# Delta net's inverse: 32x32 block products over all 128 rows, with zeros in the other rows

## The chip, the cores and the metric

The kernel runs on one core of a Trainium2 chip. The metric is the time of one execution on the device in microseconds (us). A core has five engines, each with its own instruction stream: TensorE (PE in the profile; PEld is its loading of the stationary operand), VectorE (DVE), ScalarE (ACT), GpSimd (POOL) and SyncE (SP). TensorE multiplies with a contraction over the partitions of its two operands: `pm(out, lhsT, rhs)` sums over the rows (partitions) that the slices of `lhsT` and `rhs` name, the columns of `lhsT` become the rows of `out`, and the columns of `rhs` its columns. A product "32x32 over 32 rows" therefore has 32 rows of contraction, 32 output rows and 32 output columns.

## The reference

The program is a trunk of two blocks on a sequence of 1024 rows and 1024 columns: a gated delta net and a convolutional feed-forward net, then retention and a second feed-forward net. The change lies in the delta net, which has 8 heads of 128 columns and works on chunks of 64 rows. For each head and chunk it solves a lower triangular system with a unit diagonal:

```
kk  = jnp.where(strict, jnp.einsum('bhncd,bhnmd->bhncm', kb, k) * decay, 0.0)
rhs = jnp.concatenate([v * beta[..., None], kb * jnp.exp(gc)[..., None]], axis=-1)
sol = lax.linalg.triangular_solve(kk + eye, rhs, left_side=True, lower=True, unit_diagonal=True)
u, w = sol[..., :dv], sol[..., dv:]
```

Then a scan over the 16 chunks carries a 128x128 state from chunk to chunk.

## The kernel before, in words

Two chunks of 64 rows are held as one tile of 128 rows, so a head has 8 chunk pairs, n = 0..7 (`NCH`). Heads are worked in quads (g = 0, 1, four heads) and pairs (p = 0..3, two heads). The inverse of the 64x64 triangles is built from the inside out.

`t_path(g)` makes, for the four heads of a quad, the inverses of all 32x32 diagonal blocks by 31 steps of forward substitution on DVE. They lie in two "lane" tiles, RX and TX (one the transpose of the other, block by block; L900, L904).

`t_chain(p)` (L915) then joins 32x32 blocks to 64x64 and 64x64 to 128x128 for the two heads of a pair. Its stages, which the prediction goes through:

- R, the result, is zeroed by POOL (L922), and its four diagonal blocks are copied from RX (`block`, L930 on DVE for odd p, L932 on ACT for even p; POOL L952 for the lower two).
- T0, a lane tile of 128 rows x (2 heads, 8 chunk pairs, 64 columns), gets three diagonal blocks from TX: blocks 0 and 2 into columns 0:32 and block 1 into columns 32:64 (L930 or L932). POOL zeroes the corner in rows 0:32, columns 32:64 (L937).
- First products (L960 to L965): 32 per pair, U^T times T0, 32x32 over 32 rows, into the PSUM tile `pa`. Each is fp32 and appears as two instructions in the profile, `mm<-T,U 32*32`.
- ACT copies `pa` to `xa` (L967), rows 32:64 and 96:128.
- Second products (L970 to L977): 48 per pair, `xa` with R and R with `xa`, 32x32 over 32 rows, into `pb`; for o = 0 two alternate that write different column groups of the array. In the profile they are `mm<-R,xa 32*32` and `mm<-xa,R 32*32`.
- DVE writes them, negated, into T0 (L980) and R (L984).
- Then the same with blocks of 64: products `mm<-T,U 64*64` over 64 rows, ACT's copy `xb` (L994), products `mm<-R,xb 64*64`, and R is written.

What the delta net needs around it runs between these stages: `prep(p)` (transposes of V by products with the identity, `acc<-cst,qkv` L719 on PE, L1017 on DVE), `dt_half` (`acc<-qkv` products, DVE L1046), `conv_half` (the causal convolution of a projection: ACT L485 and L488 read the PSUM accumulator, DVE L490 three taps, ACT L491 silu), the projections themselves (gemm "triples" of three 128x512 products, `acc<-hT,wl` and twice `acc<-hT,wh`), and `scan` (its steps over the chunks).

The order of the work on PE is set by a list scheduler in the program. `run(todo)` (L727) keeps a list of generators by priority. `pm` (L715) and `ptr` (L718) pin each product behind the one before it and advance a modelled clock; `yield LAT[..]` parks a generator for a modelled latency, `emit` and `after_ev` tie generators to each other, and `take` and `give` count free buffers ("lane": 4, "t2": 3, and others). Where no stage is ready, a filler (gemm triples) is issued. The order on the other engines follows from the program's dependencies by the tile scheduler, in about the order in which the operations are written.

Of the kernel before, what the change touches and what calls it, by code (L numbers as in the profile page):

```python
# [33 lines left out]
def trunk_kernel(ctx: ExitStack, tc, A):  # L34
    nc = tc.nc
    pe, act, dve, pool, sp = nc.tensor, nc.scalar, nc.vector, nc.gpsimd, nc.sync
# [9 lines left out]
    def tl(tag, shape, dt=F32, name=None):  # L46
        return sb.tile(shape, dt, tag=tag, name=name or tag, bufs=BUFS[tag])

    def two(tag, dt=F32, name=None):
        if tag in ("qkv", "auh"):  # L50
            return tl(tag, [P, HALF], dt, name), tl(tag, [P, HALF], dt, name)
        t = tl(tag, [P, 2, HALF], dt, name)
        return t[:, 0], t[:, 1]
# [7 lines left out]
    def mm_tile():  # L61
        return ps.tile([P, HALF], F32, tag="mm", name="mm", bufs=2)
# [13 lines left out]
    def v4(ap):  # L76
        return ap.rearrange("p (c f) -> p c f", f=P)
# [620 lines left out]
    U, DT, R, St = {}, {}, {}, {}  # L698
# [4 lines left out]
    events = {}  # L703

    def pq(inst, cost):
        if pin[0] is not None:
            tc.add_manual_dep(inst.ins, pin[0].name,
                              mybir.DependencyInfo(mybir.DependencyClass.NoSync, mybir.DependencyReason.DATA),
                              reason="issue order")
        pin[0] = inst.ins  # L710
        clk[0] += cost
# [3 lines left out]
    def pm(out, lhsT, rhs, start=True, stop=True, cost=None):  # L715
        pq(pe.matmul(out, lhsT, rhs, start=start, stop=stop), cost or COST[out.shape[-1]])  # L716
# [4 lines left out]
    def after_ev(*names):  # L721
        return ("ev", names)

    def emit(name, lat=0.0):
        events[name] = clk[0] + lat
# [40 lines left out]
    def q4s(q4):  # L766
        return slice(q4 * 4, (q4 + 1) * 4)
# [3 lines left out]
    def take(tag, n):  # L771
        while free[tag] < n:
            yield lambda: free[tag] >= n
        free[tag] -= n

    def give(tag, n):
        free[tag] += n
# [131 lines left out]
    def rx(h, n):  # L909
        return R[h][n // 4][:, n % 4 * P:n % 4 * P + P]  # L910
# [4 lines left out]
    def t_chain(p):  # L915
        heads = pairs[p]
        yield after_ev(("X", p // 2))
        yield from take("auh", 4)
        for h in heads:
            R[h] = two("auh", F32, "R")  # L920
            for q4 in range(2):
                pool.memset(R[h][q4], 0.0)  # L922
        yield after_ev(("T", p // 2))
        RX, TX = RTX[p // 2]
        cx = p % 2 * 16
        yield from take("lane", 1)

        def block(out, src):
            if p % 2:
                dve.tensor_copy(out, src)  # L930
            else:
                act.activation(out, src, AF.Copy)  # L932
        T0 = tl("lane", [P, 2, NCH, 64], name="T0")
        lo, hi = slice(0, 64), slice(64, 128)
        for hh, h in enumerate(heads):
            ch = slice(cx + hh * 8, cx + hh * 8 + 8)
            pool.memset(T0[0:32, hh, :, 32:64], 0.0)  # L937
            for b in range(3):
                bs = slice(32 * b, 32 * b + 32)
                cs = slice(32, 64) if b == 1 else slice(0, 32)  # L940
                block(T0[bs, hh, :, cs], TX[bs, :, ch].rearrange("p i c -> p c i"))
        for hh, h in enumerate(heads):
            for q4 in range(2):
                Rv = v4(R[h][q4])
                ch = slice(cx + hh * 8 + q4 * 4, cx + hh * 8 + q4 * 4 + 4)
                for b in range(4):
                    bs = slice(32 * b, 32 * b + 32)
                    src = RX[bs, :, ch].rearrange("p i c -> p c i")
                    if b < 2:
                        block(Rv[bs, :, bs], src)  # L950
                    else:
                        pool.tensor_copy(Rv[bs, :, bs], src)  # L952
        if ("T0", p ^ 1) in events:
            give("lane", 2)
        emit(("T0", p))
        yield LAT["T0"]
        yield from take("t2", 1)
        pa = mm_tile()
        xa = tl("t2", [P, HALF], name="xa")
        for o in (0, 64):  # L960
            l3, h3 = slice(o, o + 32), slice(o + 32, o + 64)
            for hh, h in enumerate(heads):
                for n in range(NCH):
                    c0 = hh * 256 + 32 * n
                    pm(pa[h3, c0:c0 + 32], U[h][l3, n, h3], T0[l3, hh, n, 0:32])  # L965
        for o in (0, 64):
            act.activation(xa[o + 32:o + 64], pa[o + 32:o + 64], AF.Copy)  # L967
        yield LAT["t1"]
        pb = mm_tile()
        for o in (0, 64):  # L970
            l3, h3 = slice(o, o + 32), slice(o + 32, o + 64)
            for hh, h in enumerate(heads):
                for n in range(NCH):
                    c0 = hh * 256 + 32 * n
                    pm(pb[l3, c0:c0 + 32], xa[h3, c0:c0 + 32], rx(h, n)[h3, h3])
                    if o == 0:
                        pm(pb[h3, c0:c0 + 32], rx(h, n)[h3, h3], xa[h3, c0:c0 + 32])  # L977
        for hh, h in enumerate(heads):
            pv = pb[:, hh * 256:hh * 256 + 256].rearrange("p (c f) -> p c f", f=32)
            dve.tensor_scalar(T0[32:64, hh, :, 0:32], pv[32:64], -1.0, None, ALU.mult)  # L980
            for o in (64, 0):
                l3, h3 = slice(o, o + 32), slice(o + 32, o + 64)
                for q4 in range(2):
                    dve.tensor_scalar(v4(R[h][q4])[l3, :, h3], pv[l3, q4s(q4)], -1.0, None, ALU.mult)  # L984
        give("t2", 1)
        yield LAT["t2"]
        yield from take("t2", 2)
        xb = {}
        for hh, h in enumerate(heads):
            pa = mm_tile()  # L990
            xb[h] = tl("t2", [P, HALF], name="xb")
            for n in range(NCH):
                pm(pa[hi, 64 * n:64 * n + 64], U[h][lo, n, hi], T0[lo, hh, n])
            act.activation(xb[h][hi], pa[hi], AF.Copy)  # L994
        emit(("Ufree", p))
        give("lane", 1)
        yield LAT["t3"]
        for h in heads:
            pb = mm_tile()
            for n in range(NCH):  # L1000
                pm(pb[lo, 64 * n:64 * n + 64], xb[h][hi, 64 * n:64 * n + 64], rx(h, n)[hi, hi])
            pv = pb.rearrange("p (c f) -> p c f", f=64)
            for q4 in range(2):
                dve.tensor_scalar(v4(R[h][q4])[lo, :, hi], pv[lo, q4s(q4)], -1.0, None, ALU.mult)
        give("t2", 2)
        emit(("R", p), LAT["mm"])
# [222 lines left out]
    c, z = "c", "z"  # L1229
# [5 lines left out]
    for p in range(4):  # L1235
        q = p & 2
        todo += [(q + 0.28, t_decay(p)), (q + 0.2, t_chain(p)), (q + 0.25, prep(p)), (q + 0.22, dt_half(p, 0)), (q + 0.24, dt_half(p, 1)),
                 (q + 0.0 + p % 2 * 0.1, scan(p, pairs[p][0])), (q + 0.05 + p % 2 * 0.1, scan(p, pairs[p][1]))]
# [577 lines left out]
    cs = {}  # L1816
# [358 lines left out]
```

## Time and profile before

| what | us |
|---|---|
| median of 3 runs | 2892.94 (2889.35 to 2898.21) |
| the profiled execution | 2895.01 |
| its span in the profile | 2893.2 |
| first 32x32 products, quad 0 / quad 1 | from 261.10 / from 507.09 |

The whole delta net inverse is two short stretches, one for each quad, in a span of 2893.2 us; the mean granted clock of TensorE over the span is 0.988. The views used are the page (busy shares, and the span in 40 slices, one slice being 72.3 us), the table by stretches, which gives for each stretch its length, the busy time of each engine with the number of instructions, the granted TensorE clock (PEclk, 1.00 is full speed), the DMA share and GB/s, and the waits, groups and timeline. In the table by stretches a row such as "257.64:261.05 3.41, 3.41 (x13) ..." reads: from 257.64 to 261.05, 3.41 us long, PE busy 3.41 us in 13 instructions. In groups and in the timeline, `L716` and `L719` are the two lines that issue every product here (`pm` and `ptr`), so products are told apart by the names of their tiles and their sizes. In the timeline a row has its start, its length and, in brackets, the idle time ahead of it with what ended it.

### The profile page before, as it was taken

To read this page: it belongs to the slowest core of one execution; us is meant where nothing else is said; L and a number is where in the kernel's file an instruction comes from. 1 tells how busy PE (TensorE), PEld (TensorE's weight loads), DVE (VectorE), ACT (ScalarE), POOL (GpSimd) and SP (SyncE) were. 2 spreads that over 40 slices of the span, in tenths; PEclk is the share of its full clock that TensorE was granted. 3 is DMA by queue.
4 is the path that set the end of the run, shared out by engine and by line. 5 is a ranking of instruction groups with operands and counts; after the bars stand their busy time and mean duration, and the time that the engine had idled before them with its cause. 6 is when DMAs were issued, how large, how long until landed. Compare 5 with 4: busy or idle time off the path is not lost.

```text
span 2893.2 us, 38921 instructions
## 1 busy us (share of the span) xinstructions
PE 2796.5 (97%) x13594; PEld 2289.9 (79%) x13594; DVE 2181.8 (75%) x3874; ACT 1296.7 (45%) x2387; POOL 484.6 (17%) x509
## 2 busy tenths in 40 slices
PE   7999999999999999999999999999999999999997
PEld 6788887887787777887788887777777788888886
DVE  5787688576788888858687666666789887777779
ACT  4664375344544444545443333222344644444543
POOL 0311231010022333000000001333301023332001
PEclk9998999899999999999999999999999999999999
DMA  7233233174254655845443354665764253434853
GB/s 277 84 99 117 89 129 112 44 241 153 83 179 169 204 181 176 294 150 175 150 142 113 131 197 143 203 188 177 233 221 150 73 197 138 142 132 161 289 182 116
DMA packets 252884, 465.30 MB, mean 161 GB/s; under 512 B 24144, under 2 KB 77776, under 8 KB 252688
## 3 DMA queue, kind: packets, MB, share of 16 engines
q1 hardware_dynamic: 218560, 408.02, 42.8%
q10 hardware_dynamic: 31488, 46.15, 4.3%
q0 software_dynamic: 2640, 8.65, 0.8%
q8 instruction: 107, 1.75, 0.2%
q14 instruction: 89, 0.73, 0.1%
HBM read 346.86 MB, written 115.87 MB: 160 GB/s over the span
## 4 chain that ended last, share of the span: by engine, by line
PE 60%; DVE 21%; DMA 8%; issue 5%; ACT 4%; POOL 1%; SPq 0%; ACTq 0%; DVEq 0%; POOLq 0%
PE acc L716 11%; PE acc L1292 5%; PE acc L1592 4%; PE sc L716 4%; PE acc L110 4%; PE acc L111 4%; PE acc L112 4%; PE mm L716 3%; PE sc L1292 3%; DVE o L1738 2%; DVE wb L90 2%; DMA wr<-in_ffn_up 2%; DMA mvw<-in_ada_w 2%; DVE mm L1346 2%; DVE ada L239 1%
## 5 line engine op out<-in xcount | busy, mean ns | idle before, releaser
L716 PE MATMUL acc<-hT,wh 128*128 128x512 f32 x960 | 301.1, 395 | 0.0
L1592 PE MATMUL acc<-bb,ab 128*128 128x512 f32 x984 | 231.0, 394 | 8.2 <-DVE ab L90 4.4
L89 ACT ACTIVATE ab<-ar 128x512 fp32r<-128x512 f32 x210 | 131.4, 630 | 222.9 <-PE mm L303 49.8
L1592 PEld LDWEIGHTS acc<-bb,ab 128*128 128x128 f32 x984 | 184.2, 189 | 50.0 <-DVE bb L90 4.7
L716 PEld LDWEIGHTS acc<-hT,wh 128*128 128x128 f32 x960 | 183.2, 191 | 36.1
L90 DVE TENSOR_TENSOR ab<-ar,ab 128x512 fp32r<-128x512 f32 x210 | 146.1, 701 | 80.3 <-ACT ab L89 80.1
L1292 PE MATMUL acc<-T,wb 128*128 128x512 f32 x840 | 202.0, 389 | 0.4 <-DVE wb L90 0.4
L716 PE MATMUL acc<-hT,wl 128*128 128x512 f32 x480 | 197.4, 411 | 3.3 <-ACT sq L509 2.1
L89 ACT ACTIVATE wb<-mm 128x512 fp32r<-128x512 f32 x216 | 124.3, 597 | 167.8 <-DVE mm L1346 154.1
L1292 PEld LDWEIGHTS acc<-T,wb 128*128 128x128 f32 x840 | 157.5, 188 | 33.8 <-ACT o L1739 1.2
L90 DVE TENSOR_TENSOR wl<-wr,wh 128x1024 fp32r<-128x1024 f32 x98 | 122.8, 1253 | 76.3 <-ACT wh L89 76.0
L90 DVE TENSOR_TENSOR wb<-wr,wb 128x512 fp32r<-128x512 f32 x162 | 116.3, 719 | 66.1 <-ACT wb L89 66.1
L89 ACT ACTIVATE wh<-wr 128x1024 fp32r<-128x1024 f32 x98 | 103.8, 1060 | 137.4 <-PE acc L716 54.1
L1769 POOL TENSOR_TENSOR o<-o 128x512 f32<-128x512 f32 x80 | 113.0, 1422 | 265.2 <-ACT pc L1362 173.1
L1738 DVE SCALAR_TENSOR_TENSOR o<-g,vc,o 128x512 f32<-128x512 f32 (+2 forms) x176 | 148.3, 852 | 8.2 <-ACT o L1733 7.0
L90 DVE TENSOR_TENSOR wb<-mm,wb 128x512 fp32r<-128x512 f32 x216 | 144.4, 681 | 7.6 <-ACT wb L89 7.6
L89 ACT ACTIVATE wb<-wr 128x512 fp32r<-128x512 f32 x162 | 101.2, 626 | 94.8 <-PE acc L1292 28.5
L1346 DVE TENSOR_TENSOR mm<-wr 128x512 f32<-128x512 f32 x108 | 85.9, 796 | 75.5 <-DMA wr<-in_ffn_up 60.9
L716 PE MATMUL acc<-wh,hT 128*128 128x512 f32 x384 | 134.3, 412 | 1.8 <-DVE vv L90 1.8
L1362 ACT ACTIVATE pc<-acc 128x512 f32<-128x512 f32 x143 | 84.3, 590 | 109.9 <-PE acc L1292 63.4
L239 DVE SCALAR_TENSOR_TENSOR ada<-mvw,e,ada 128x512 f32<-128x512 f32 x140 | 105.3, 752 | 23.4 <-DMA mvw<-in_ada_w 23.0
L110 PE MATMUL acc<-T,wb 128*128 128x512 f32 x292 | 114.4, 392 | 6.1 <-DVE wb L90 6.1
(674 smaller groups left out, 7371.9 us busy)
## 6 DMA issues: line engine op xcount, KB each, us to landing
wr<-in_ffn_up SPq DMA_DIRECT2D x92, 512.0 KB, 3.9
mvw<-in_ada_w SPq DMA_DIRECT2D x80, 512.0 KB, 4.3
ad<-o SPq DMA_DIRECT2D x154, 256.0 KB, 2.3
ar<-ad SPq DMA_DIRECT2D x154, 256.0 KB, 3.9
Br<-in_ffn_down SPq DMA_DIRECT2D x88, 256.0 KB, 3.6
wr<-in_ret_wv SPq DMA_DIRECT2D x32, 512.0 KB, 3.7
ar<-od SPq DMA_DIRECT2D x56, 256.0 KB, 5.2
wr<-in_gdn_wqkv SPq DMA_DIRECT2D x24, 512.0 KB, 3.6
```

What stands on the lines that cost most here:

```text
L89: anchor["sp"] = act.activation(dst_h, src, AF.Copy)
L90: eng.tensor_tensor(dst_l, src, dst_h, ALU.subtract)
L110: mm(acc, wl[:, k], hl[0], start=first, stop=False)
L111: mm(acc, wh[:, k], hl[1], start=False, stop=False)
L112: mm(acc, wh[:, k], hl[0], start=False, stop=last)
L239: dve.scalar_tensor_tensor(a, wr[:, kk], e[:, k:k + 1], a, ALU.mult, ALU.add)
L716: pq(pe.matmul(out, lhsT, rhs, start=start, stop=stop), cost or COST[out.shape[-1]])
L1292: return pe.matmul(*a, skip_group_check=True, **kw)
L1346: dve.tensor_tensor(t, x, y, op)
L1592: return pe.matmul(*args, skip_group_check=True, **kw)
L1738: dve.scalar_tensor_tensor(tv, gv[:, c0 - j:c1 - j], w[:, 2 - j:3 - j], tv, ALU.mult, ALU.add)
L1769: (dve if fp == 0 else pool).tensor_tensor(o[d], o[x], o[y], op)
```

## The change

T0 is zeroed whole, 128 rows, by POOL. Before the first products only blocks 0 and 2 are copied into it, block 0 into columns 0:32 and block 2 into columns 32:64. With that, the first products run over all 128 rows of U and T0: the rows of T0 that a product is not to see hold zeros in the columns that it uses. `xa` is zeroed whole by POOL (a new instruction for each pair), and ACT then fills the rows that it filled before. The second products run over all 128 rows of `xa` and R, with the zeros in `xa`. Block 1 of T0 (rows 32:64, columns 32:64) is copied behind the first products and ACT's copies, and the event "T1", with the return of two lane buffers, comes after it.

```diff
         for hh, h in enumerate(heads):
             ch = slice(cx + hh * 8, cx + hh * 8 + 8)
-            pool.memset(T0[0:32, hh, :, 32:64], 0.0)
-            for b in range(3):
+            pool.memset(T0[:, hh], 0.0)
+            for b in (0, 2):
                 bs = slice(32 * b, 32 * b + 32)
-                cs = slice(32, 64) if b == 1 else slice(0, 32)
-                block(T0[bs, hh, :, cs], TX[bs, :, ch].rearrange("p i c -> p c i"))
+                block(T0[bs, hh, :, 16 * b:16 * b + 32], TX[bs, :, ch].rearrange("p i c -> p c i"))
...
-        if ("T0", p ^ 1) in events:
-            give("lane", 2)
         emit(("T0", p))
...
         xa = tl("t2", [P, HALF], name="xa")
+        pool.memset(xa, 0.0)
         for o in (0, 64):
-            l3, h3 = slice(o, o + 32), slice(o + 32, o + 64)
+            h3 = slice(o + 32, o + 64)
...
-                    pm(pa[h3, c0:c0 + 32], U[h][l3, n, h3], T0[l3, hh, n, 0:32])
+                    pm(pa[h3, c0:c0 + 32], U[h][:, n, h3], T0[:, hh, n, o // 2:o // 2 + 32])
         for o in (0, 64):
             act.activation(xa[o + 32:o + 64], pa[o + 32:o + 64], AF.Copy)
+        for hh in range(2):
+            ch = slice(cx + hh * 8, cx + hh * 8 + 8)
+            block(T0[32:64, hh, :, 32:64], TX[32:64, :, ch].rearrange("p i c -> p c i"))
+        if ("T1", p ^ 1) in events:
+            give("lane", 2)
+        emit(("T1", p))
...
-                    pm(pb[l3, c0:c0 + 32], xa[h3, c0:c0 + 32], rx(h, n)[h3, h3])
+                    pm(pb[l3, c0:c0 + 32], xa[:, c0:c0 + 32], rx(h, n)[:, h3])
                     if o == 0:
-                        pm(pb[h3, c0:c0 + 32], rx(h, n)[h3, h3], xa[h3, c0:c0 + 32])
+                        pm(pb[h3, c0:c0 + 32], rx(h, n)[:, h3], xa[:, c0:c0 + 32])
```

The change also moves instructions, since the modelled clock and the buffer counts see it. On PE, in quad 0, the rows just ahead of the first products change as follows; `T_2178` is T0 of pair 0, `T_2203` (before) and `T_2201` (now) is T0 of pair 1, `acc<-qkv` are the products of `dt_half`, and `acc<-cst,qkv` the transposes of V.

```order
 L716 MATMUL acc<-hT,wh 128x512 x2
-L716 MATMUL acc<-qkv 128x128 x4
+L716 MATMUL acc<-hT,wl 128x512
+L716 MATMUL acc<-hT,wh 128x512 x2
+L719 MATMUL acc<-cst,qkv 128x128 x8
+L716 MATMUL acc<-hT,wl 128x512
+L716 MATMUL acc<-hT,wh 128x512 x2
 L716 MATMUL mm<-T_2178,U 32x32 x32
-L716 MATMUL mm<-T_2203,U 32x32 x32
+L716 MATMUL mm<-T_2201,U 32x32 x32
```

Four `dt_half` products leave this place, and two gemm triples and eight transposes come to it; the `dt_half` products stand further down, between the second products and the 64x64 products.

On ACT, at the same place in the program (quad 0, pair 0), the copies of T0's blocks and the convolution's steps stand as follows; `oq` is the convolution's output.

```order
 L488 ACTIVATE oq<-acc,vc 128x512
-L932 ACTIVATE T_2178<-TX 32x8x32 x6
 L491 ACTIVATE oq<-oq 128x512
-L1212 DMA qd<-oq 128x512
+L932 ACTIVATE T_2178<-TX 32x8x32 x2
+L1216 DMA qd<-oq 128x512
+L932 ACTIVATE T_2178<-TX 32x8x32 x2
+L491 ACTIVATE oq<-oq 128x512
 L485 ACTIVATE raw<-acc 128x512
 L488 ACTIVATE oq<-acc,vc 128x512
```

Where six copies stood ahead of the convolution's steps there are four, with a silu and the issue of a store among them; the two others come later, one ahead of each pair's copies of `xa`.

On ACT in quad 1, pair 2 (`T_4595` before and `T_4597` now are its T0), the same copies stand ahead of L251, which makes the shift and scale `ada` and frees its accumulator. Before, the rows there are these.

```order
L932 ACTIVATE T_4595<-TX 32x8x32 x5
L485 ACTIVATE raw<-acc 128x512
L488 ACTIVATE qkv<-acc,vc 128x512
L932 ACTIVATE T_4595<-TX 32x8x32
L491 ACTIVATE qkv<-qkv 128x512
L485 ACTIVATE raw<-acc 128x512
L488 ACTIVATE qkv<-acc,vc 128x512
L89 ACTIVATE wh<-wr 128x1024
L251 ACTIVATE ada,cs<-acc 128x128 x4
```

With the change they are these.

```order
L485 ACTIVATE raw<-acc 128x512
L488 ACTIVATE qkv<-acc,vc 128x512
L491 ACTIVATE qkv<-qkv 128x512
L932 ACTIVATE T_4597<-TX 32x8x32 x4
L485 ACTIVATE raw<-acc 128x512
L488 ACTIVATE qkv<-acc,vc 128x512
L89 ACTIVATE wh<-wr 128x1024
L251 ACTIVATE ada,cs<-acc 128x128 x4
```

The first L485, L488 and L491 come ahead of the copies, and four copies instead of six stand ahead of L251.

## The prediction

> **What bounds the kernel now.** I read the page first, for the engine that sets the span and for the clock of TensorE.
>
> ```profile
> span 2893.2 us, 38921 instructions
> PE 2796.5 (97%) x13594; PEld 2289.9 (79%) x13594; DVE 2181.8 (75%) x3874; ACT 1296.7 (45%) x2387; POOL 484.6 (17%) x509
> PEclk9998999899999999999999999999999999999999
> ```
>
> PE is busy for 97% of the span, so a microsecond taken out of PE's row, busy or idle, mostly leaves the span too; what becomes late on another engine counts only where it leaves PE idle. The second thing to see is the digit 8 in two of the 40 slices, the 4th and the 8th (216.9 to 289.3 and 506.3 to 578.6 us): there TensorE was granted less than its full clock for a while, and there the two quads do the products that the change rewrites. So I cut these places into stretches at the points where the clock changes, which turn out to lie 3.41 us apart.
>
> ```profile
> core 0: us, PE busy (x) PEld busy (x) DVE busy (x) ACT busy (x) POOL busy (x), PEclk, DMA share, GB/s
> 254.23:257.64 3.41, 0.99 (x7) 0.91 (x8) 2.28 (x4) 2.85 (x5) 0.00 (x0) 1.00 0.73 207
> 257.64:261.05 3.41, 3.41 (x13) 2.85 (x11) 3.18 (x5) 0.42 (x1) 0.00 (x0) 0.50 0.70 260
> 261.05:264.45 3.40, 3.40 (x116) 3.35 (x116) 1.76 (x3) 1.18 (x2) 0.00 (x0) 1.00 0.60 189
> 264.45:267.87 3.42, 3.42 (x29) 3.21 (x26) 1.26 (x2) 1.81 (x3) 0.00 (x0) 0.50 0.52 200
> 267.87:271.28 3.41, 3.41 (x171) 3.06 (x170) 1.02 (x4) 0.00 (x0) 0.00 (x0) 1.00 0.43 145
> 271.28:281.52 10.24, 9.56 (x76) 8.57 (x74) 6.63 (x21) 1.18 (x2) 0.00 (x0) 0.50 0.17 57
> 284.93:288.35 3.42, 3.42 (x49) 3.25 (x48) 1.05 (x3) 1.18 (x2) 0.00 (x0) 1.00 0.07 28
> 506.79:510.20 3.41, 3.41 (x111) 3.24 (x110) 1.09 (x3) 2.61 (x11) 0.00 (x0) 1.00 0.02 5
> 510.20:530.68 20.48, 19.80 (x282) 18.13 (x279) 8.91 (x25) 2.58 (x5) 0.00 (x0) 0.50 0.09 28
> ```
>
> Each row's clock answers to the row above it. After the nearly idle 254.23 to 257.64 (PE busy 0.99 of 3.41) comes a window at 0.50. But after 261.05 to 264.45, in which PE was busy all the time, comes a window at 0.50 as well, and so again after 267.87 to 271.28 and after 506.79 to 510.20. What those three share is over 100 small instructions: the 32x32 products. They keep PE busy and are followed by half a clock, as if PE had idled. Wider work does not do this: 284.93 to 288.35, most of it 64x64 products, stays at 1.00. So the clock seems to follow how much of the array works, and a 32x32 product over 32 rows counts as next to nothing. In 271.28 to 281.52 and 510.20 to 530.68 the same half clock lasts for three and for six windows.
>
> Last, the waits of PE, first around quad 0 (250 to 300), then around quad 1 (484 to 600).
>
> ```profile
> PE acc L719 <- ACT oq L488: 4.2, 1, 4.2
> ...
> PE acc L716 <- ACT ada L251: 1.1, 1, 1.1
> ...
> PE sc L716 <- ACT qkv L1079: 0.6, 1, 0.6
> ...
> PE sc L716 <- DVE qkv L1097: 0.3, 1, 0.3
> ```
>
> **The change part by part.** All sums are against the profiled execution's 2895.0 us (span 2893.2 and 1.8 around it).
>
> **(a) Copies of T0 that leave ACT's and DVE's queues.** This is the chain behind PE's wait of 4.2 us in quad 0.
>
> ```profile
> 249.25 4.00 ACT L932 ACTIVATE T<-TX 32x256 f32<-32x256 f32 x6 [1.20 <-DVE TX L904]
> 250.61 2.96 DVE L930 COPY T<-TX 32x256 f32<-32x256 f32 x6
> 254.38 0.63 ACT L491 ACTIVATE oq<-oq 128x512 f32<-128x512 f32 x1 [1.12 <-DVE oq L490]
> 255.42 0.60 ACT L485 ACTIVATE raw<-acc 128x512 f32<-128x512 f32 x1 [0.41 <-ACT oq L491]
> 255.91 0.68 ACT L488 ACTIVATE oq<-acc,vc 128x512 f32<-128x512 f32 x1
> 256.65 0.66 PE L719 MATMUL acc<-cst,qkv 128*128 128x128 f32 x4 [4.24 <-ACT oq L488]
> ```
>
> PE waits for ACT's L488, which stands behind L485 and L491, which waits for DVE's taps, which wait behind six copies on DVE. With the change four copies stand there, on each engine. Two copies fewer on DVE are 2 x 0.494 = 1.0 us, by the group below; ACT's own two are 1.33 us. The chain ends about 1.0 us sooner; PE's two extra triples ahead of it (front, first order piece) could hide up to 1.4 us more, and DVE has two more transposed V tiles to write. I take **1.0 gained**, between 0 and 2.4.
>
> ```profile
> L932 ACT ACTIVATE T<-TX 32x256 f32<-32x256 f32 x12 | 8.0, 666 | 2.1 <-DVE TX L904 2.0
> L930 DVE COPY T<-TX 32x256 f32<-32x256 f32 x12 | 5.9, 494 | 0.2
> ```
>
> In quad 1 PE waits 1.1 us for L251. Two copies fewer ahead of L251 are 2 x 0.666 = 1.33 us, more than the wait: **1.1 gained**, between 0 and 1.1. The copies that move come back behind the first products, two per pair. There they have cover: ACT waits 5.18 us for the first products in quad 0 and DVE 2.38 us ahead of L980 (below), and PE has transposes and a triple between first and second products. Were the cover gone, it would be 0.67 us for each of two quads.
>
> **(b) Clock.** If products over 128 rows count as full work, the half clock goes where 32x32 products brought it. These stretches of it are bound by PE alone:
>
> ```profile
> 265.30:267.87 2.57, 2.57 (x12) 2.42 (x11) 1.26 (x2) 1.18 (x2) 0.00 (x0) 0.50 0.39 147
> 276.31:281.52 5.21, 5.21 (x28) 4.80 (x29) 1.79 (x3) 0.59 (x1) 0.00 (x0) 0.50 0.30 104
> 511.43:514.29 2.86, 2.86 (x14) 2.53 (x12) 0.69 (x1) 1.18 (x2) 0.00 (x0) 0.50 0.02 6
> 514.29:517.35 3.06, 3.06 (x96) 3.06 (x96) 0.69 (x1) 0.00 (x0) 0.00 (x0) 0.50 0.00 0
> 524.10:530.68 6.58, 6.28 (x31) 5.59 (x32) 1.55 (x3) 0.84 (x2) 0.00 (x0) 0.50 0.25 82
> ```
>
> At full clock wide products take half: 2.57, 5.21, 2.86 and 6.58 us become 1.3, 2.6, 1.4 and 3.3 (savings 1.3, 2.6, 1.4, 3.3). The second products of pair 2, 96 instructions in 3.06 us, go at the rate of 267.87 to 271.28 (3.41 us for 171, 20 ns each): 1.9 us, 1.1 saved. The rest of the first products, 510.20 to 511.43, is 1.23 us long and saves not quite half, 0.5. Together **10.2 gained**. The window 257.64 to 261.05 stays at half clock: it follows an idle gap, which shrinks but remains.
>
> Between these stretches the half clock is free, since DVE sets the pace:
>
> ```profile
> 270.37 0.42 DVE L980 TENSOR_SCALAR T<-mm 32x256 f32<-32x256 f32 x1 [2.38 <-PE mm L716]
> ...
> 275.14 0.98 DVE L984 TENSOR_SCALAR R<-mm 32x128 f32<-32x128 f32 x4
> 276.31 1.97 PE L716 MATMUL mm<-T,U 64*64 64x64 f32 x16 [0.68 <-ACT xb L994]
> ```
>
> From 270.37 to 276.12 DVE works without a gap, and the 64x64 products of the second head follow it. So I count nothing there.
>
> **(c) A window that cools all the same.** With a full clock PE comes through that stretch sooner than DVE and idles. Its work there, some 6 us at half clock, needs about 3 at full, and I reckon with 1.9 us of idle time in each quad. If, in one of two quads, this falls into one window together with 64x64 products, the next 3.4 us may run at half: **1.7 lost**, between 0 and 3.4.
>
> **(d) The other order.** The program's scheduler puts 22 gemm triples instead of 25 between the scan steps of quad 1, the three others elsewhere. A triple is 0.68 us:
>
> ```profile
> 235.28 0.39 PE L716 MATMUL acc<-hT,wl 128*128 128x512 f32 x1
> ...
> 235.96 0.39 PE L716 MATMUL acc<-hT,wl 128*128 128x512 f32 x1
> ```
>
> PE waits in that scan only 0.6 + 0.3 us now (rows of waits above). With 2.0 us less filler it waits between 0 and 2.0 longer: **1.0 lost**. Further, the loads for `dt_half` start later, because the lane buffers return at T1; their products, too, now stand behind the second products, and I count nothing.
>
> **(e) POOL and the products themselves.** Whole memsets take POOL longer.
>
> ```profile
> L922 POOL MEMSET R<- 128x512 f32 x16 | 8.1, 527 | 79.3 <-ACT t L601 59.8 <-PE mm L584 12.2 <-PE acc L716 6.2
> L937 POOL MEMSET T<- 32x256 f32 x8 | 2.6, 357 | 0.2
> ```
>
> Eight by 0.17 us more and four new ones by 0.53 us are 3.5 us on an engine that is busy for 17%; none stands ahead of something PE waits for, so nothing. That a product over 128 rows costs no more than one over 32 is not shown for this shape; the nearest rows are weight loads.
>
> ```profile
> L716 PEld LDWEIGHTS mm<-T,U 32*32 32x32 f32 x256 | 8.4, 114 | 0.4 <-issue 0.4
> L614 PEld LDWEIGHTS sc<-hT,wab 128*32 128x32 f32 x8 | 0.9, 108 | 1.7 <-DVE hT L90 1.4
> 283.30 2.08 PE L716 MATMUL mm<-R,xb 64*64 64x64 f32 x32
> ```
>
> 32 columns over 128 rows load in 108 ns, over 32 rows in 114: the rows don't matter to the load. I take nothing, with the 64x64 rate (2.08 us for 32, 65 ns) as the other end, which gives the slower rival.
>
> The sum: 1.0 + 1.1 + 10.2 - 1.7 - 1.0 = 9.6 us gained, 2885.4 against the profiled execution. That one stands 2.1 above the median of the runs; against the median it is 2892.9 - 9.6 = **2883.3 us**. This case's own range: with (c) and (d) at nothing 2880.6, with (a) at its upper end too 2879.2; with both at their worst (3.4 and 2.0) and (a) at nothing, 2888.1.
>
> **The rivals.** First, **the clock falls anyway**. The rows cannot separate rows of the array in use from its columns or its cells: a 128x32 product fills 4 of 16 blocks of 32x32, as a 64x64 one does, but only 32 columns; and the rows added hold zeros, which may count as nothing. Then (b) and (c) go, and 2.1 us less 0 to 2.0 remain: 2890.8 to 2892.9, about 2892. Against it stands 284.93 to 288.35, where products on a quarter of the array keep 1.00. The same comes out if only the idle time of PE moves the clock, since no idle time goes but (a).
>
> The Trainium skill, "TensorE: Matmul & The Clock Gate", Part 1, has such a rule: a monitor sets the clock by how busy TensorE was in a free-running window of about 3.4 us, and goes to half after an idle one. The window agrees with the 3.41 us between the edges above; "busy" does not, as PE was busy for 3.40 of 3.41 us before windows at 0.50. Read to the letter, that page would have this change leave the clock alone, and the result be this rival's.
>
> Second, **slower: the 128-row products themselves**. Products over 32 rows leave the other rows of the array to the next weight load; products over all rows may not let load and product, or two column groups, run beside each other. At full clock a first one takes 29 ns now (3.40 us for 116, from 261.05) and the second ones 20 on the mean (171 from 267.87); a third of these is plain, so at 29 for the plain ones an alternating one takes 15.5. At the 64x64 rate of 65 ns, the 256 first ones cost 36 more (9.2 us), the 128 plain second ones likewise (4.6), and the 256 alternating ones 49.5 more (12.7): 26.5 us, so 2883.3 + 26.5 = 2909.8 with the clock kept up. It decides from 15 ns on each of 640 instructions, which eats up 9.6 us. For it speaks that alternating ones gain from two groups today; against it, that the load does not grow with rows.
>
> **How the numbers follow.** A measurement of this kernel can tell about 0.3%, 8.7 us, from no change: faster is below 2884.3, slower above 2901.6. The forecast has 0.57: 0.44 of it faster, 0.13 within, as its range straddles 2884.3. The clock that falls anyway has 0.25: within, but for 0.02 on each side. Dearer products have 0.15: 0.13 slower, 0.02 within. The other 0.03 is an order of the scan that loses or gains more than (d): 0.01 faster, 0.02 slower. That makes faster 0.47, within 0.36, slower 0.17. The range goes from 2877, below the forecast's own end by the runs' scatter, to 2897, above the first rival by the same; the dearer products and the tails are left out.
>
> **What would show it.** Right, if the windows behind the 32x32 products, which are then 128*32, are granted 1.00, if they take no more than 29 ns each, if PE's wait for L488 falls to about 3, and if slices 4 and 8 read 9. Windows at 0.50 behind full windows of these products mean the first rival; products above 40 ns at a clock of 1.00 mean the second. New waits of PE between the steps of the scan of quad 1 show (d), and a single window at 0.50 behind 276 or 524 shows (c). Wrong would be the whole sum if the products keep the clock and the end still does not move: then DVE's chain sets more of both stretches than I took.

## The result

The changed kernel takes 2877.0 us (median of 7 runs, 2869.75 to 2887.71) against 2893.84 for the kernel before in the same comparison. The ratio is 0.9939, with a 95% interval of 0.9921 to 0.9957: 12 to 23 us faster. A second comparison, below, gave 0.9956 (0.9941 to 0.997), 9 to 17 us. The forecast was 9.6 us; the sign was right and the clock is where the gain comes from, but the size was too small.

The page of the changed kernel answers to the three lines that opened the prediction.

```profile
span 2868.4 us, 38930 instructions
PE 2780.8 (97%) x13594; PEld 2273.7 (79%) x13594; DVE 2177.9 (76%) x3874; ACT 1298.0 (45%) x2387; POOL 499.8 (17%) x513
PEclk9999999999999999999999999999999999999999
```

PE has as many instructions as before and is busy for 15.7 us less; POOL has 15 us more. No slice of the clock's row reads 8 any more. The stretches of the changed kernel, cut at its own windows, around quad 0 and then around quad 1:

```profile
core 0: us, PE busy (x) PEld busy (x) DVE busy (x) ACT busy (x) POOL busy (x), PEclk, DMA share, GB/s
250.00:253.41 3.41, 0.66 (x6) 0.67 (x7) 0.64 (x2) 3.37 (x6) 1.25 (x4) 0.99 0.44 133
253.41:256.76 3.35, 3.35 (x33) 2.60 (x32) 3.26 (x7) 0.23 (x1) 0.00 (x0) 0.50 0.75 261
256.76:260.17 3.41, 3.41 (x110) 3.37 (x108) 3.28 (x7) 2.52 (x5) 0.00 (x0) 1.00 0.48 155
260.17:263.59 3.42, 3.42 (x119) 3.00 (x119) 1.41 (x3) 1.77 (x3) 0.00 (x0) 1.00 0.50 144
263.59:267.00 3.41, 3.29 (x112) 3.09 (x102) 3.18 (x11) 0.00 (x0) 0.00 (x0) 1.00 0.33 119
267.00:270.41 3.41, 2.73 (x38) 2.52 (x37) 3.10 (x12) 1.19 (x2) 0.00 (x0) 1.00 0.38 130
...
502.53:505.94 3.41, 3.41 (x179) 3.41 (x172) 1.62 (x6) 0.00 (x0) 0.00 (x0) 1.00 0.37 124
505.94:509.35 3.41, 2.61 (x33) 2.27 (x30) 3.26 (x13) 0.59 (x1) 0.00 (x0) 1.00 0.00 0
```

One window at 0.50 is left, 253.41 to 256.76, behind the idle gap. Windows full of 128x32 products (256.76, 502.53) are followed by 1.00. The longest waits of PE where the prediction looked for them are these, first in quad 0, then in quad 1 with its scan.

```profile
PE acc L719 <- ACT oq L488: 2.9, 1, 2.9
...
PE mm L716 <- ACT qkv L1083: 2.7, 2, 1.7
```

The wait for L488 is shorter, the one for L251 is gone, and in the scan PE waits 2.7 us for L1083, where the kernel before waited 1.6 us for the same line (its L1079).

Where the time went: I aligned the products of both traces one by one and cut them at common products, from the transposes of V ahead of quad 0's stall to a product of the stage behind the scan (L327). That is one stretch in each kernel; the experiments below are read by it too. The first rows are of the kernel before, in two profiles, the last two of the changed kernel, in two profiles.

```profile
251.81:635.56 383.75, 366.78 (x2789) 320.67 (x2788) 272.84 (x682) 182.15 (x427) 63.50 (x91) 0.95 0.35 117
```

```profile
248.80:639.54 390.74, 371.56 (x2790) 324.56 (x2788) 274.11 (x682) 183.17 (x428) 63.97 (x93) 0.93 0.34 115
```

```profile
246.77:616.41 369.64, 353.74 (x2796) 307.85 (x2795) 273.92 (x685) 186.00 (x431) 66.27 (x96) 1.00 0.36 120
```

```profile
247.85:619.38 371.53, 353.45 (x2797) 307.81 (x2796) 276.17 (x687) 185.70 (x431) 67.92 (x99) 1.00 0.35 119
```

Between the two profiles that the comparison is about, the stretch gives 383.75 - 369.64 = 14.1 us: 13.0 of it PE busy time (366.78 to 353.74), 1.1 idle time. Taken over two profiles each, it is 387.2 - 370.6 = 16.7 us. The work in the stretch is not quite the same: four `dt_half` products, 0.9 us on PE, stand just ahead of it in the kernel before (250.92 to 251.81) and inside it in the changed one. For equal work the gain is 15.0 us, and 17.6 over two profiles each.

The spans differ by 24.8 us; the other 10.7 lie outside the stretch. 5.0 of them come before it: 0.9 are those four products, and for the rest the first profile of before had 10.2 us of half clock between 42 and 60 us, the changed kernel's first profile none there, its second 6.8. The other 5.7 come behind it and are idle time of PE. The part behind the stretch took 2257.6 us before, and 2252.0 and 2256.8 in the two profiles of the changed kernel. So both parts differ between runs of one kernel, and I count neither as part of the change.

### The profile page after: what moved, and what is told of

Same layout as the page of the kernel before. It is cut to its first block, busy times and chain, and to the rows that moved or that the text cites. A ratio compares the mean times of both kernels' runs of the same rounds, so it can differ in the third digit from the quotient of the medians.

```text
span 2868.4 us, 38930 instructions
## 1 busy us (share of the span) xinstructions
PE 2780.8 (97%) x13594; PEld 2273.7 (79%) x13594; DVE 2177.9 (76%) x3874; ACT 1298.0 (45%) x2387; POOL 499.8 (17%) x513
## 4 chain that ended last, share of the span: by engine, by line
PE 61%; DVE 20%; DMA 9%; ACT 5%; issue 4%; POOL 1%; SPq 0%; ACTq 0%; DVEq 0%; POOLq 0%
PE acc L716 11%; PE acc L1296 6%; PE acc L110 5%; PE acc L111 4%; PE acc L112 4%; PE sc L716 4%; PE sc L1296 3%; PE acc L1596 3%; PE mm L716 2%; DVE o L1742 2%; DVE wb L90 2%; PE sc L110 2%; PE sc L112 2%; PE sc L111 2%; DMA mvw<-in_ada_w 1%
## 5 line engine op out<-in xcount | busy, mean ns | idle before, releaser
L1773 POOL TENSOR_TENSOR o<-o 128x512 f32<-128x512 f32 x80 | 126.2, 1586 | 266.4 <-ACT pc L1366 173.1
```

Of the source, the lines that this page charges most:

```text
L1773: (dve if fp == 0 else pool).tensor_tensor(o[d], o[x], o[y], op)
```

## The experiments

**Order alone.** The changed kernel with products over 32 rows.

```diff
-                    pm(pa[h3, c0:c0 + 32], U[h][:, n, h3], T0[:, hh, n, o // 2:o // 2 + 32])
+                    pm(pa[h3, c0:c0 + 32], U[h][o:o + 32, n, h3], T0[o:o + 32, hh, n, o // 2:o // 2 + 32])
...
-                    pm(pb[l3, c0:c0 + 32], xa[:, c0:c0 + 32], rx(h, n)[:, h3])
+                    pm(pb[l3, c0:c0 + 32], xa[h3, c0:c0 + 32], rx(h, n)[h3, h3])
...
-                        pm(pb[h3, c0:c0 + 32], rx(h, n)[:, h3], xa[:, c0:c0 + 32])
+                        pm(pb[h3, c0:c0 + 32], rx(h, n)[h3, h3], xa[h3, c0:c0 + 32])
```

> The changed kernel with its order, its copies and its zeros as they are, but the first and second products run over 32 rows again, as before. From the transposes of V ahead of the stall in quad 0 to the first product of the norm behind the scan, the kernel before takes 383.75 us and the changed one 369.64. Theory (the gain is the clock, which follows the rows of the array in use): windows full of these products are followed by 0.50 again, some 20 to 34 us of half clock in the two quads, and the stretch takes 379 to 384 us; the time is that of before within 0.3%. Rival (the gain comes from the order and from the copies that left ACT's and DVE's queues): the stretch takes 369 to 374 us, and the time is about 0.5% below before.

The ratio to before is 1.001 (0.9997 to 1.0023): nothing is gained. The stretch, and the windows of quad 1:

```profile
247.04:633.68 386.64, 368.96 (x2797) 322.17 (x2796) 274.56 (x684) 185.69 (x431) 66.54 (x96) 0.95 0.33 114
```

```profile
505.89:509.31 3.42, 2.75 (x79) 2.62 (x80) 1.95 (x4) 2.35 (x16) 0.00 (x0) 1.00 0.02 5
509.31:516.13 6.82, 6.82 (x103) 6.01 (x102) 1.38 (x2) 2.30 (x4) 0.00 (x0) 0.50 0.01 2
516.13:519.55 3.42, 3.42 (x169) 3.38 (x163) 1.76 (x6) 0.00 (x0) 0.00 (x0) 1.00 0.02 5
519.55:529.79 10.24, 9.56 (x53) 8.63 (x54) 5.76 (x18) 1.19 (x2) 0.00 (x0) 0.50 0.15 54
```

The half clock is back behind the windows of 32x32 products, 41.0 us of it in the two quads (13.7 and 10.2 in quad 0, 6.8 and 10.2 in quad 1). The stretch of 386.64 is 2.6 us above what was expected and lies between the two profiles of the kernel before. So order, copies and zeros bring nothing that can be seen. The rows bring 386.64 - 369.64 = 17.0 us, here with the same order and so with the same work.

**One half each.** The changed kernel with 128 rows in the first products alone (the second ones edited as above), then in the second products alone (the first ones edited as above).

> The changed kernel with 128 rows in the first products only; the second products run over 32 rows. Theory: the first products keep the clock; the second ones (192 instructions in a quad, some 3.6 us, about one window) bring half clock back for one or two windows behind each quad's second products, and the stretch takes 370 to 376 us. Rival (order and copies): no change against the changed kernel, 369.6. A second rival, that only products with zeros in the moving operand count as full: no window at 0.50 behind the first products, none or one behind the second ones.

> The changed kernel with 128 rows in the second products only; the first products run over 32 rows. Theory: the 128 instructions of the first products of a quad (some 3.4 us) bring half clock for one or two windows behind them, which end once the second products have filled a window; the stretch takes 371 to 377 us. Rival (order and copies): 369.6 us and no new window at 0.50.

First products alone over 128 rows: 374.27 us, 4.6 above the changed kernel. Second products alone: 381.36 us, 11.7 above it. The theory's range held for the first and was exceeded in the second. The windows of quad 0 with the first products alone show something the expectation did not:

```profile
267.51:270.92 3.41, 3.29 (x112) 3.08 (x103) 3.17 (x11) 0.00 (x0) 0.00 (x0) 1.00 0.42 138
270.92:274.33 3.41, 1.63 (x29) 1.53 (x27) 2.97 (x11) 0.59 (x1) 0.00 (x0) 1.00 0.40 148
274.33:277.75 3.42, 3.42 (x20) 3.30 (x18) 0.86 (x2) 0.59 (x1) 0.00 (x0) 0.50 0.44 156
```

The 32-row second products (267.51) are followed by 1.00; eight 128x128 products stand in the same window, which may be why. The one that cools is the next: PE busy 1.63 of 3.41 us, with 64x64 products and a wait of 1.8 us for DVE's L988. That is term (c) of the prediction, met here and not in the changed kernel.

**64 rows.** The changed kernel with `U[h][o:o + 64, n, h3]`, `T0[o:o + 64, ...]`, `xa[o:o + 64, ...]` and `rx(h, n)[o:o + 64, h3]`.

> The changed kernel with 64 rows in both kinds of products: the 64 rows that hold the block and its neighbour, so half of the added zeros go. If the clock asks for a share of the array between 1/16 (32x32, cooled) and 1/4 (128x32, kept), this 1/8 tells on which side: theory A (the clock counts rows, and 64 of 128 are enough, as with the 64x64 products): no window at 0.50 but the one behind the idle gap, and a stretch of 369 to 371 us. Theory B (it counts cells, and 1/8 is too little): 0.50 behind full windows, 376 to 384 us.

The ratio is 0.9984 (0.9972 to 0.9997) and the stretch 380.70 us, within theory B's range. But the windows of quad 1 do not all read as B has it:

```profile
502.29:505.71 3.42, 2.43 (x67) 2.29 (x69) 2.12 (x5) 2.62 (x17) 0.00 (x0) 1.00 0.02 5
505.71:512.53 6.82, 6.82 (x95) 6.01 (x93) 1.54 (x3) 2.35 (x4) 0.00 (x0) 0.50 0.01 2
512.53:515.95 3.42, 3.42 (x183) 3.42 (x180) 1.43 (x6) 0.00 (x0) 0.00 (x0) 1.00 0.03 5
515.95:519.36 3.41, 2.61 (x36) 2.27 (x33) 3.27 (x12) 0.59 (x1) 0.00 (x0) 1.00 0.00 0
```

The 64x32 first products cool from a window that PE fills to 2.43 of 3.42 us. The second ones, also 64x32 but alternating two column groups (183 instructions in a window), keep the clock. In quad 0, where the first products begin at half clock behind the idle gap, the clock comes back only at 266.77:

```profile
256.53:266.77 10.24, 10.24 (x145) 8.87 (x145) 5.56 (x9) 2.99 (x5) 0.00 (x0) 0.50 0.34 122
266.77:270.19 3.42, 3.42 (x183) 3.42 (x184) 1.31 (x5) 0.00 (x0) 0.00 (x0) 1.00 0.47 161
```

With 128 rows the half clock ended there after one window (253.41 to 256.76). So 64 rows are near the border, how full a window is counts with the rows, and whether cells or rows are counted stayed open here.

**The change once more.** No edit.

> The changed kernel once more, unchanged, to narrow its time and to see in a second profile which differences to before return. Theory (the change acts between the stall in quad 0 and the end of the scan of quad 1, and takes 14.1 us there; the rest of the 24.8 us between the two profiled spans is half-clock windows elsewhere that differ from run to run): this stretch takes 369 to 371 us again, the parts outside it differ by several us from the first profile, and the ratio to before is 0.994 to 0.996. Rival (part of the gain comes from elsewhere in the program and is real): the parts outside repeat the first profile within 1 us, and the ratio is 0.991 to 0.993.

2875.52 us against 2889.87, ratio 0.9956 (0.9941 to 0.997), and the stretch is 371.53 us, 0.5 above what was expected. The part ahead of it took 1.1 us more than in the first profile, and the part behind it 4.8 more, so outside the stretch the first profile was a good one.

**The kernel before once more, and its order with the second products alone.** The second kernel is the kernel before with `pool.memset(xa, 0.0)`, `xa[:, ...]` and `rx(h, n)[:, h3]`.

> The kernel before once more, unchanged, for a second profile of the stretch between the stall in quad 0 and the norm behind the scan (383.75 us in the first profile, with 37.5 us of half clock). Theory: the phase of the windows moves the half clock a little, and the stretch takes 381 to 386 us. Rival (the first profile of before was an unlucky one): it takes less than 378 us.

> The kernel before, in its own order on TensorE, with xa zeroed and 128 rows in the second products only; the first ones run over 32 rows. Theory (the clock alone): the windows at 0.50 behind the second products go in part, those behind the first ones stay, and the stretch takes 376 to 381 us against 383.75. Rival (the order brings the gain): 383 to 385 us.

The kernel before took 390.74 us, 4.7 more than expected, with 51.2 us of half clock between 251 and 283 and between 511 and 535, against 37.5 in its first profile: with nothing changed, the stretch moves by 7 us from one profile to the next. With 128 rows in the second products and the old order the stretch is 381.05 us, at the upper end of the theory's range, and equal to the same half in the new order (381.36). That is the second sign that the order matters little.

**What the clock counts, first try.** The changed kernel with extra products ahead of each pair's first ones, overwritten by them; 32 moving columns. The two kernels differ in `rr, cc`: 64x64 and 32x128 (quad 0 and quad 1), and 32x64 and 64x128.

```diff
+        rr, cc = (64, 64) if p < 2 else (32, 128)
+        for rep in range(8):
+            for hh, h in enumerate(heads):
+                for n in range(NCH):
+                    c0 = hh * 256 + 32 * n
+                    pm(pa[0:cc, c0:c0 + 32], U[h][0:rr, n, 0:cc], T0[0:rr, hh, n, 0:32], cost=0.0001)
```

> The changed kernel with extra products ahead of each pair's first products, overwritten by these: in quad 0 512 instructions over 64 rows and 64 columns of the array, in quad 1 512 over 32 rows and all 128 columns, both with 32 moving columns, so that each fills some 3 windows of 3.41 us with one shape. It tells what the clock counts. Both shapes use a quarter of the array, as the 128x32 products do. Counting cells (rows times columns): 1.00 behind the windows of both. Counting rows: 0.50 behind the 32 rows, and for 64 rows as with the 64-row products of 32 columns, 0.50. Counting columns would have cooled the 128x32 products and is out already. The time is not compared: the extra work is some 26 us.

> As the probe with 64x64 and 32x128, with 32 rows and 64 columns in quad 0 (an eighth of the array) and 64 rows and 128 columns in quad 1 (a half). Counting cells: 0.50 behind the windows of the 32x64 products, 1.00 behind those of 64x128. Counting rows: 0.50 behind both, as behind the 64x32 products. The time is not compared.

All four shapes ran at half clock: those of quad 0 began at it, behind the idle gap, and did not end it, and those of quad 1 cooled. This tells nothing between rows and cells, and the groups of the first kernel show a likely reason (window 255 to 720):

```profile
L716 PEld LDWEIGHTS mm<-T,U 32*128 32x128 f32 x512 | 102.7, 310 | 0.2 <-issue 0.2
...
L716 PE MATMUL mm<-T,U 64*64 64x32 f32 x512 | 55.0, 291 | 0.0
```

512 instructions took 103 us with 128 columns and 55 with 64, 201 and 107 ns each, nearly all at half clock. The loads were busy for 102.7 of the 103.0 us: loading the stationary operand, longer with more columns, set the pace. A product with 32 moving columns was then, I take it, streaming for a part of that time only. The extra time was some 60 us in quad 0 and 106 to 109 in quad 1 instead of 26 in all.

**What the clock counts, second try.** As before, but with 512 moving columns: `pm(pa[0:cc, :], U[heads[rep % 2]][0:rr, rep, 0:cc], T0[0:rr, rep % 2].rearrange("p n c -> p (n c)"), cost=0.0001)`, eight per pair; 64x32 and 32x128 in the first kernel, 32x64 and 64x64 in the second.

> The changed kernel with extra products ahead of each pair's first products, overwritten by these, now with 512 moving columns instead of 32, so that the loading of the stationary operand does not set their pace: 32 instructions in a quad of some 430 ns, about four windows. In quad 0 over 64 rows and 32 columns of the array (an eighth of its cells, half of its rows), in quad 1 over 32 rows and 128 columns (a quarter of the cells, a quarter of the rows). Counting cells: 0.50 behind the first and 1.00 behind the second. Counting rows: 0.50 behind the second, since the 32-row products cool, and the first, with half of the rows, cools like the 64x32 products.

> As the probe before, with 32 rows and 64 columns in quad 0 (an eighth of the cells, a quarter of the rows) and 64 rows and 64 columns in quad 1 (a quarter of the cells, half of the rows). Counting cells: 0.50 behind the first, 1.00 behind the second. Counting rows: 0.50 behind both, since 64 rows by 32 columns cooled.

The first kernel, quad 0 (64x32) and quad 1 (32x128); few instructions in a window (x9) are the 512-column ones, 55 to 73 are for the most part 128x32 ones.

```profile
255.84:269.49 13.65, 13.65 (x18) 2.55 (x16) 5.15 (x10) 0.63 (x1) 0.00 (x0) 0.50 0.43 154
269.49:272.90 3.41, 3.41 (x55) 2.71 (x55) 0.00 (x0) 0.10 (x1) 0.00 (x0) 0.50 0.00 0
272.90:276.32 3.42, 3.42 (x21) 1.15 (x19) 0.00 (x0) 2.37 (x4) 0.00 (x0) 1.00 0.00 0
276.32:279.73 3.41, 3.41 (x9) 0.86 (x8) 0.00 (x0) 0.00 (x0) 0.00 (x0) 1.00 0.00 0
279.73:283.14 3.41, 3.41 (x73) 2.81 (x72) 0.87 (x3) 0.69 (x2) 0.00 (x0) 1.00 0.02 5
...
535.73:539.14 3.41, 3.41 (x14) 1.66 (x12) 0.00 (x0) 1.91 (x4) 0.00 (x0) 1.00 0.02 5
539.14:549.38 10.24, 10.24 (x64) 5.11 (x64) 0.14 (x1) 0.00 (x0) 0.00 (x0) 0.50 0.00 0
```

The second kernel, quad 0 (32x64) and quad 1 (64x64):

```profile
256.35:259.76 3.41, 3.41 (x9) 1.03 (x9) 3.22 (x6) 0.10 (x1) 0.00 (x0) 1.00 0.49 163
259.76:270.00 10.24, 10.24 (x74) 4.80 (x72) 0.00 (x0) 1.17 (x2) 0.00 (x0) 0.50 0.20 77
...
526.00:529.41 3.41, 3.41 (x9) 1.06 (x8) 0.17 (x1) 0.09 (x1) 0.00 (x0) 1.00 0.00 0
529.41:532.83 3.42, 3.42 (x65) 2.11 (x64) 0.00 (x0) 0.20 (x1) 0.00 (x0) 1.00 0.00 0
```

Compare windows that PE fills wholly at 1.00. Behind 32x64 (256.35) and 32x128 (535.73) comes 0.50, behind 64x64 (526.00) and 64x32 (276.32) comes 1.00. These are one or two windows of each shape, in one run each. 32x128 and 64x64 use the same number of cells, a quarter of the array, and 64x32 half as many: the cells are out, and the columns with them. What separates the windows is the rows. The expectation of "counting rows" was wrong in its threshold: half of the rows is enough to keep the clock where the products fill the window. It is not enough to bring it back: at 0.50, 13.65 us of 64x32 products stay at 0.50, and it takes a window that is mostly 128x32 ones (269.49) to return to 1.00.

**A try at the stall that is left.** `"T": 6.0` raised to 7.0 in the table of modelled latencies, meant to bring a silu and two reads of an accumulator ahead of T0's copies on ACT.

> The changed kernel with the modelled latency behind the triangles' last step raised from 6.0 to 7.0, so that a silu and the convolution's two reads of the accumulator stand ahead of T0's copies on ACT, and two more gemm triples ahead of the first products on PE. If ACT's copies waiting for TX are what holds the convolution up, PE's wait of 2.9 us for L488 falls to between 0 and 1.5, the half-clock window behind it goes, and the stretch takes 365 to 369 us against 369.6. Rival: DVE's taps hold it up, the wait stays at 2 to 3 us, and the stretch takes 369 to 372 us.

A miss: the ratio is 1.0015 (1.0004 to 1.0027), and the stretch 377.31 us, above both ranges. Two waits of PE in quad 0, and two at the end of the stretch, show why:

```profile
PE acc L719 <- DVE qkv L1021: 4.1, 1, 4.1
PE acc L719 <- ACT oq L488: 1.8, 1, 1.8
```

```profile
PE acc L719 <- DVE qkv L1120: 4.4, 1, 4.4
PE mm L1799 <- DVE dg L1798: 2.7, 1, 2.7
```

The wait for L488 fell to 1.8 us, above the 1.5 of the expectation, but not for the reason given there. In quad 0 ACT does the same as in the changed kernel up to L488 (a silu, four copies of T0, a silu, L485), and L488 starts at 252.11 us against 252.01. PE has two triples more ahead of the wait and so comes to it later. What holds the convolution up was therefore not tested. A wait of 4.1 us for DVE came beside it; the modelled clock also moved work out of the stretch (2770 instructions on PE against 2796) and opened gaps at its end, with 10.2 us of half clock (614.65 to 624.89). The changed kernel remains the fastest of all that ran.

## Why the prediction was too small

Right, by its own steps:

- The mechanism: PE is the bound, and the clock follows how much of the array products use. Order alone, at 1.001, against the change, at 0.994 to 0.996, shows it. That it is the rows, the prediction had left open; the probes with 512 moving columns say so.
- **(e)**: 128-row products cost hardly more. 128 first products of quad 1 take 3.94 us, 31 ns each (29 before), and 192 second ones 3.95 us, 21 ns each (20 before). Both rivals fail, the first by the clock, the second by these rates. POOL's memsets of T0 and xa take 4.0 and 2.1 us where T0's took 2.6, the 3.5 more that were forecast; the rest of POOL's 15 us are other work's spans.

**(a)** came out in its number by luck. PE's wait for L488 was 4.2 and 5.2 us in two profiles of before and is 2.9 and 4.5 in two of the change, on the mean 1.0 less, as forecast. But with the same order and the same copies it was 4.4, 3.2, 4.6 and 4.1 us in the four kernels with fewer rows, so the moved copies alone do not shorten it. The wait of 1.1 us for L251 is gone in both profiles of the change. It is there, with 1.3 us, in the three of those kernels whose first products run over fewer rows, so the copies alone do not remove it.

The step that failed is in **(b)**: "Between these stretches the half clock is free, since DVE sets the pace." It left out 271.28 to 276.31 and 517.35 to 524.10, 11.8 of the 34.1 us of half clock that the change removed; half of that, 5.9 us, is missing from the sum. The prediction saw that DVE works there without a gap, and took the second head's 64x64 products for its successors. The row that it quoted names ACT's `xb`, not DVE, and 0.68 us of idle time in all. What stands on PE there, in quad 1 before and with the change:

```profile
521.75 1.97 PE L716 MATMUL mm<-T,U 64*64 64x64 f32 x16
524.40 1.97 PE L716 MATMUL mm<-T,U 64*64 64x64 f32 x16 [0.68 <-ACT xb L994]
```

```profile
507.28 1.11 PE L716 MATMUL mm<-T,U 64*64 64x64 f32 x16
509.07 1.14 PE L716 MATMUL mm<-T,U 64*64 64x64 f32 x16 [0.68 <-ACT xb L998]
```

And DVE's chain with the change:

```profile
504.27 0.42 DVE L984 TENSOR_SCALAR T<-mm 32x256 f32<-32x256 f32 x1 [1.89 <-PE mm L716]
...
509.04 0.98 DVE L988 TENSOR_SCALAR R<-mm 32x128 f32<-32x128 f32 x4
```

DVE takes as long as before, 5.75 us. But the 64x64 products of pair 2 need only its first half, pair 2's own writes; those of the second head wait for `xb`, ACT's copy, which waits for the first head's products, and these ran at half clock. So 64x64 products of pair 2 take 1.1 us a head instead of 2.0, the second head's start at 509.07 while DVE is still busy until 510.0, and from the first second product to there it is 6.95 us (from 502.12) instead of 10.1 (from 514.29). Of these 3.2 us the prediction had counted 1.1, for the second products.

What that was worth: with the order held, 37.6 us of half clock went (41.0 less 3.4), and 17.0 us with it, 0.45 us for each. By the halves, 0.5, the 34.1 us would give 17.1; the prediction took 10.2 from 21.5 of them. The 17.0 also hold what the clock does to waits of PE, such as that for L251.

**(c)** and **(d)** did not come, and that is 2.7 us more. No window cooled a second time, though two came to 2.73 and 2.61 us of busy time; with fewer rows elsewhere, or another phase, such windows did cool in the halves above (with the second products alone, one with 2.62 us busy, from 275.19). That none did here may be luck. In the scan, which lost three triples (2.0 us of work), the time fell from 82.52 to 80.04 us, and PE's idle time in it from 4.1 to 3.4 us; the wait of 2.7 us takes the place of others. The 0.6 + 0.3 us that the prediction read as the scan's waits end at 600 us, in the middle of the scan, which goes on to 635.6.

With 17.0 for the clock and nothing for (a), (c) and (d) the sum would have been 17.0, against 15.0 and 17.6 measured in the stretch for equal work. It can't be settled closer, as two profiles of the kernel before differ by 7 us. The medians of the two comparisons differ by 17 and 14 us.

The Trainium skill, "TensorE: Matmul & The Clock Gate", Part 1, by which the clock asks how busy TensorE was, does not hold as it stands, with busy as the profile counts it: TensorE was busy for 3.41 of 3.41 us at 535.73 in the 32x128 products, and the next windows were at 0.50.

## What to carry to other kernels

Small products over 32 rows that keep TensorE busy can still halve its clock for what follows, wide work included: look for rows of 0.50 behind full windows. Rows of zeros in one operand kept the clock here and cost next to nothing on TensorE (31 ns against 29 for a first product), with an engine that had time to write the zeros. And when an engine works without a gap beside a slow one, follow what the waiting instruction itself names, before calling the slow one free.

## What the runs showed of the hardware

In these traces the clock changes between windows of 3.41 us, and each window's clock answers to the work of the one before it. At full clock, in windows that PE filled wholly, 32 rows (with 32, 64 or 128 columns) led to 0.50, and 64 and 128 rows (64x32, 64x64, 128x32) to 1.00. At half clock 64x32 did not bring 1.00 back and 128x32 did. A window with 64-row products and gaps cooled (2.43 of 3.42 us busy). Where the limit lies between 32 and 64 rows, and how rows and gaps add up, was not measured. And the time to load a stationary operand grew with its columns: products with 32 moving columns took 107 ns each with 64 columns and 201 with 128, nearly all at half clock.
